# Two lots of the down projection as seven block products, with the sums on GpSimd

## The chip, the cores and the metric

The kernel runs on one core of one Trainium2 chip. The metric is the device time of one execution, in microseconds (us). Before the change the median of three runs is 1117.38 us (1116.92 to 1117.68). The engines are called as in the profile: PE (TensorE, matmuls), PEld (its weight loads), DVE (VectorE), ACT (ScalarE), POOL (GpSimd) and SP (SyncE, which issues the transfers).

## The reference

Two layers of a bidirectional encoder on 512 tokens of width 1024. A layer has a mixer (12 token heads and 4 heads over 256 memory rows) and a gated feed-forward part with 2816 hidden columns. The change lies in the second.

```python
for i in range(DEPTH):                      # DEPTH = 2; mixer a, then mixer b
    h = rms_norm(x, g_mix_pre[i])
    ...                                     # attention heads, tok and mo
    o = jnp.concatenate([tok, mo], axis=-1) @ w_o[i]
    x = x + rms_norm(o, g_mix_post[i])
    h = rms_norm(x, g_ffn_pre[i])
    gu = h @ w_gate_up[i]                   # (512, 1024) @ (1024, 5632)
    f = (jax.nn.silu(gu[..., :D_FF]) * gu[..., D_FF:]) @ w_down[i]   # (512, 2816) @ (2816, 1024)
    x = x + rms_norm(f, g_ffn_post[i])
```

## The kernel before

**Numbers in two parts.** Every float32 operand of a matmul is split into a high part (rounded, on ACT) and a low part (the rest, on DVE: source minus high part). A product is three matmuls, high x high, high x low and low x high. `split` is this pair of instructions, lines 283 and 287.

**Hidden tiles.** A tile `f` is 128 of the 2816 hidden columns, for all 512 tokens, so a layer has 22. Tiles 0 and 1 are multiplied plainly. The other 20 are made by `body`, with seven block products instead of eight: gate and up weights are the two columns of a 2x2 block matrix, and the tokens fall into two halves of 256. A product is 12 matmuls of 256 columns (line 1026 to 1028), 84 a tile. The products are called A11, A12, S2, nS1, S3, S4, A22, after the forms of the activations, which `Forms.finish` makes once a layer. The weights' forms are made for each tile: `raw` holds the gate block, `rb` the up block, `ru` sums. Pair `a` is split from the gate block as loaded. `load_b` and `prep_c` make three sums of 128x512 (lines 1004, 1005, 1010) and split pair `c`, `prep_b` splits pair `b`, and `prep_d` makes a fourth sum (line 1017) and splits pair `d`. All four sums are on DVE.

**Order in a body.** PE works through S2 and nS1 (pair c of this tile), A11 of the next tile (pair a), S3 (b), A12 of the next tile, S4 (b), A22 (d). Between them ACT copies intermediate sums out of PSUM (`u2`, `p5`, `p1`), and DVE adds them (`c`, lines 1062 and 1070). At the end come silu, the product `s*c` (line 1076) and its split into the hidden tile `f` (lines 1078, 1079).

**Lots and the way down.** Tiles come in lots of 8, 6 and 8. When a lot's tiles stand in SBUF, `down` multiplies them with their rows of `w_down`: for both column halves of 512, for each unit of two tiles (128x1024, split as loaded), for all four token tiles of 128, six matmuls of 512 columns (`down_prod`). Sums of a lot go from PSUM to `o`, by an ACT copy for the first lot and a DVE sum afterwards. The last body of a lot has no next tile, so the first unit of the way down fills those two places (`first`, `second`). The last lot's way down is in `ffn_out`, with the closing norm and the residual. In layer 1 the last token tile's second half is done in two parts of 256 columns (`ending`).

**Buffers and queues.** Split weights lie in a ring of four pairs (`whl`), loaded ones in three `raw`, two `rb` and two `ru` buffers. The order on PE is that of the code; those of the other engines are set by a scheduler when the program is built, and each engine works strictly in that order. SP issues the loads, each waiting for its buffer. `ahead`, called after each unit of `down`, uses idle time to split a weight of layer 1's mixer and to store the pair, by turns a load and a store: eight pairs are wanted, four of `wq` and four of `wo`, and 14 calls in layer 0 make seven in time.

Of the kernel before, what the change touches and what calls it, by code (L numbers as in the profile page):

```python
# [35 lines left out]
LOTS = ((0, 8), (8, 14), (14, 22))  # L36
# [146 lines left out]
class Trunk:  # L183
# [703 lines left out]
    def ffn_out(self, get, w, fs, o, head, gpost, gpre, resid, dst, rs):  # L887
# [14 lines left out]

        def ending(t):

# [3 lines left out]
            for z in range(2):  # L908
                ps = self.tagged(("acc", "s")[z])[:, :256]
                for u in range(nu):  # L910
                    for k in (2 * u, 2 * u + 1):
                        c = slice((k % 2) * 512 + 256 * z, (k % 2) * 512 + 256 * z + 256)
                        self.mm3(ps, get(0, k, t), get(1, k, t), wu[u][0][:, c], wu[u][1][:, c], k == 0, k == len(fs) - 1)
# [383 lines left out]
```

## Time and profile before

| what | value |
| --- | --- |
| median of three runs | 1117.38 us |
| span of the profiled execution | 1115.4 us |
| PE busy | 1094.4 us, 98% |
| DVE busy | 839.4 us, 75% |
| ACT busy | 661.2 us, 59% |
| POOL busy | 201.4 us, 18% |
| mean granted clock of TensorE | 0.998 |
| transfers | 139.30 MB, mean 125 GB/s |

The page gives the span from first to last instruction and no further time for the profiled execution; the span lies 2.0 us below the runs' median. A row of a timeline has the start and the duration in us, engine, line, operation, output<-inputs and shapes; what stands in brackets is idle time before it and what ended that. A row of a group ends with busy us and mean ns of one, then the idle time before. A busy PE is not PE at its peak, because matmuls overlap in the record.

### The profile page before, as it was taken

The numbers are of one execution on the slowest core, as the hardware profiler recorded it, in microseconds if no ns is written. First come the engines' busy times: TensorE is split into PE (matmuls) and PEld (weight loads), VectorE is DVE, ScalarE is ACT, GpSimd is POOL, SyncE is SP. The second block draws the span as 40 slices with busy tenths as digits, with TensorE's granted clock in tenths as the row PEclk, the third lists the DMA queues.
The fourth block names the chain that finished last, engine by engine and source line by source line (L and its number), as shares of the span: only waits on it lengthen the run. The fifth ranks groups of instructions, "written<-read, shape, count | busy, mean of one in ns | idle before, by whom it ended". The sixth has DMA issues, their size and how long they took to land.

```text
span 1115.4 us, 19564 instructions
## 1 busy us (share of the span) xinstructions
PE 1094.4 (98%) x7487; PEld 1005.2 (90%) x7487; DVE 839.4 (75%) x1401; ACT 661.2 (59%) x1349; POOL 201.4 (18%) x349
## 2 busy tenths in 40 slices
PE   9999999999999999999999999999999999999997
PEld 7889988999889989998898888878999899899986
DVE  5688886899557866885797988758996478669854
ACT  7578984766445534653467888756664356346631
POOL 5693341102000000000343553212000000000001
PEclk9999999999999999999999999999999999999999
DMA  6521025443653382326443221145136123423243
GB/s 239 189 79 51 25 77 189 152 152 115 238 188 112 113 286 76 100 79 210 162 169 114 77 76 39 38 152 188 44 111 225 57 85 114 141 68 101 83 166 114
DMA packets 38686, 139.30 MB, mean 125 GB/s; under 512 B 4416, under 2 KB 4800, under 8 KB 38464
## 3 DMA queue, kind: packets, MB, share of 16 engines
q1 hardware_dynamic: 38448, 137.91, 36.7%
q8 instruction: 59, 0.97, 0.4%
q14 instruction: 35, 0.29, 0.1%
q10 hardware_dynamic: 144, 0.14, 0.0%
HBM read 119.16 MB, written 18.87 MB: 124 GB/s over the span
## 4 chain that ended last, share of the span: by engine, by line
PE 86%; DVE 5%; POOL 3%; ACT 3%; issue 2%; DMA 1%; SPq 0%; DVEq 0%; POOLq 0%; ACTq 0%
PE ps L274 13%; PE ps L275 13%; PE ps L273 13%; PE ps L1028 12%; PE ps L1026 12%; PE ps L1027 12%; PE tp L631 3%; PE o L646 2%; PE o L645 2%; PE s L570 1%; PE s L571 1%; DVE tl L287 1%; DMA raw<-in_wkv_dram 1%; POOL p L621 1%; POOL r L307 1%
## 5 line engine op out<-in xcount | busy, mean ns | idle before, releaser
L283 ACT ACTIVATE whi<-raw 128x1024 fp32r<-128x1024 f32 (+2 forms) x186 | 157.8, 862 | 174.0 <-PE ps L1028 73.7
L287 DVE TENSOR_TENSOR wlo<-raw,whi 128x1024 fp32r<-128x1024 f32 (+2 forms) x178 | 175.3, 996 | 74.5 <-ACT whi L283 70.6
L1027 PE MATMUL ps<-sf,wlo 128*128 128x256 f32 x640 | 179.7, 281 | 0.0
L1026 PE MATMUL ps<-sf,whi 128*128 128x256 f32 x640 | 179.7, 281 | 0.0
L1028 PE MATMUL ps<-sf,whi 128*128 128x256 f32 x640 | 179.7, 281 | 0.0
L273 PE MATMUL ps<-whi,f 128*128 128x512 f32 (+1 forms) x360 | 138.6, 385 | 0.0
L274 PE MATMUL ps<-wlo,f 128*128 128x512 f32 (+1 forms) x360 | 138.5, 385 | 0.0
L275 PE MATMUL ps<-whi,f 128*128 128x512 f32 (+1 forms) x360 | 138.4, 384 | 0.0
L1028 PE MATMUL ps<-a,whi 128*128 128x256 f32 x480 | 134.4, 280 | 0.0
L1026 PE MATMUL ps<-a,whi 128*128 128x256 f32 x480 | 134.3, 280 | 0.0
L1027 PE MATMUL ps<-a,wlo 128*128 128x256 f32 x480 | 133.8, 279 | 0.0
L1027 PEld LDWEIGHTS ps<-sf,wlo 128*128 128x128 f32 x640 | 121.4, 190 | 0.5
L1026 PEld LDWEIGHTS ps<-sf,whi 128*128 128x128 f32 x640 | 121.1, 189 | 0.5
L1028 PEld LDWEIGHTS ps<-sf,whi 128*128 128x128 f32 x640 | 121.4, 190 | 0.0
L316 POOL TENSOR_SCALAR e<-sso 128x1 f32<-128x1 f32 x8 | 3.4, 422 | 563.6 <-ACT junk L311 563.5
L273 PE MATMUL ps<-whi,hT 128*128 128x256 f32 (+1 forms) x320 | 98.7, 309 | 0.4 <-ACT whi L300 0.4
L274 PE MATMUL ps<-wlo,hT 128*128 128x256 f32 (+1 forms) x320 | 93.9, 294 | 2.1 <-DVE wlo L287 1.3
L621 POOL TENSOR_SCALAR p<-p,rd 128x256 f32<-128x256 f32 (+2 forms) x128 | 76.7, 618 | 99.6 <-DVE rd L618 44.8
L275 PE MATMUL ps<-whi,hT 128*128 128x256 f32 (+1 forms) x320 | 93.7, 293 | 0.0
L1027 PEld LDWEIGHTS ps<-a,wlo 128*128 128x128 f32 x480 | 90.5, 188 | 0.2
L1026 PEld LDWEIGHTS ps<-a,whi 128*128 128x128 f32 x480 | 90.5, 188 | 0.2
L1028 PEld LDWEIGHTS ps<-a,whi 128*128 128x128 f32 x480 | 90.1, 188 | 0.0
(205 smaller groups left out, 2738.0 us busy)
## 6 DMA issues: line engine op xcount, KB each, us to landing
raw<-in_wgu_dram SPq DMA_DIRECT2D x48, 512.0 KB, 4.4
raw<-in_wd_dram SPq DMA_DIRECT2D x44, 512.0 KB, 4.4
rb<-in_wgu_dram SPq DMA_DIRECT2D x40, 512.0 KB, 3.6
raw<-in_wo_dram SPq DMA_DIRECT2D x17, 512.0 KB, 3.6
raw<-in_wq_dram SPq DMA_DIRECT2D x16, 512.0 KB, 4.7
xt<-x SPq DMA_DIRECT2D x12, 512.0 KB, 4.4
raw<-in_wm_dram SPq DMA_DIRECT2D x8, 512.0 KB, 3.9
x<-y SPq DMA_DIRECT2D x8, 512.0 KB, 2.9
```

The costliest lines, as they stand in the source:

```text
L273: mm(out, lh, rh, start=first, stop=False)
L274: mm(out, lh, rl, start=False, stop=False)
L275: mm(out, ll, rh, start=False, stop=last)
L283: a = nc.scalar.activation(hi, src, AF.Copy)
L287: b = nc.vector.tensor_sub(lo, src, hi.bitcast(F32))
L621: self.pooled = nc.gpsimd.tensor_scalar(hd["p"][z][:, :n], hd["p"][z][:, :n], rd[:, z:z + 1], 1.0, op0=OP.mult, op1=OP.mult)
L631: nc.tensor.transpose(tp[:, z], hd["p"][i][:, jj * P:(jj + 1) * P], self.ident)
L645: nc.tensor.matmul(o[:, c0:c1], hd["v"](j), th, start=(j == 0), stop=False, skip_group_check=True)
L646: nc.tensor.matmul(o[:, c0:c1], hd["v"](j), tl, start=False, stop=last, skip_group_check=True)
L1026: mm(out, wh[:, s], rh, start=start and k == 0, stop=False, skip_group_check=True)
L1027: mm(out, wl[:, s], rh, start=False, stop=False, skip_group_check=True)
L1028: mm(out, wh[:, s], rl, start=False, stop=k == 3, skip_group_check=True)
```

## The change

Lots have 6, 6 and 10 tiles. For the first two lots the way down is a 2x2 block product of its own: tokens in halves of 256, the lot's tiles in halves of three (`HALF`), the output's columns in halves of 512. Seven products take the place of eight, each of 18 matmuls of 512 columns. In the order of the work they are A11, A12, S2, S1, S3, S4 and A22.

The hidden tiles are needed in more forms. `keep_hidden` stores tiles of a lot's first half as first token half and, negated, a difference (one POOL subtraction of 128x256, line 990). For a tile of the second half POOL makes three sums of 128x256 (lines 997 to 999), which are split as two forms more. The weight blocks are `b11`, `b12`, `b21` and `b22` (128x1536, held as 1024 + 512); `t2` is a fifth buffer for sums. POOL makes the four block sums (`sub`, line 1164). Each product's block is split by `pairs`. `down_begin` stands in the place of `first`, with four of the six steps of A11.

The four sums of gate and up weights for each tile (lines 1048, 1049, 1054, 1061) are issued on POOL instead of DVE. `ahead` is called six times a lot, 12 in all. `ffn_out` now works on ten tiles, and does the first unit of its second half for all token tiles before it loads the last one. The negation of hidden tiles, which body had before, is now in the plain tiles too (`signed`).

```diff
-LOTS = ((0, 8), (8, 14), (14, 22))
+LOTS = ((0, 6), (6, 12), (12, 22))
+HALF = 3
...
-    def down(self, get, w, fs, c, o, head=None):
...
-        wu = [self.unit(w[1, fs[0] // 2 + u]) for u in range(nu)]
+        wu = [self.unit(w[1, u]) for u in range(nu - 1)]
...
+        wu.append(self.unit(w[1, nu - 1]))
...
-        def hidden(i):
+        def slots(i):
             return [f32r(pools["f"], [P, S], f"f{z}{i}") for z in range(2)]
+        def signed(pair, c, src):
+            nc.scalar.activation(pair[0][:, c], src, AF.Copy, scale=-1.0)
+            nc.vector.scalar_tensor_tensor(pair[1][:, c], src, -1.0, pair[0][:, c].bitcast(F32), op0=OP.mult,
+                                           op1=OP.subtract)
+        def keep_hidden(f, s):
+            lot = next(c for c, (f0, f1) in enumerate(LOTS) if f0 <= f < f1)
+            i = f - LOTS[lot][0]
+            p = F[f] = slots(i)
+            a, b = slice(0, 256), slice(256, 512)
+            if lot == len(LOTS) - 1:
+                signed(p, slice(0, 512), s)
+            elif i < HALF:
+                signed(p, a, s[:, a])
+                nc.gpsimd.tensor_tensor(s[:, a], s[:, a], s[:, b], op=OP.subtract)
+                signed(p, b, s[:, a])
+                kept[i] = s
+            else:
+                signed(p, slice(0, 512), s)
+                r = kept.pop(i - HALF)
+                x = temp("q")
+                nc.gpsimd.tensor_tensor(x[:, b], s[:, b], r[:, a], op=OP.subtract)
+                nc.gpsimd.tensor_tensor(x[:, a], s[:, b], r[:, b], op=OP.add)
+                nc.gpsimd.tensor_tensor(r[:, a], s[:, a], x[:, b], op=OP.subtract)
+                F["S12", lot, i - HALF] = v = slots(i + HALF)
+                signed(v, slice(0, 512), x)
+                if (i - HALF) % 2 == 0:
+                    F["S4", lot, (i - HALF) // 2] = slots(3 * HALF + (i - HALF) // 2)
+                q = i - HALF
+                signed(F["S4", lot, q // 2], (a, b)[q % 2], r[:, a])
+        def block(c, name, z, i, t):
+            f0 = LOTS[c][0]
+            key, h = {"A11": (f0 + i, 0), "S3": (f0 + i, 1), "A12": (f0 + HALF + i, 0), "A22": (f0 + HALF + i, 1),
+                      "S1": (("S12", c, i), 0), "S2": (("S12", c, i), 1), "S4": (("S4", c, i // 2), i % 2)}[name]
+            pair = F[key]
+            return pair[z][:, 256 * h + P * t:256 * h + P * t + P]
         def temp(tag, n=512):
-            return tmp.tile([P, n], F32, tag=tag, name=tag, bufs=2 if n == 512 else 1)
+            return tmp.tile([P, n], F32, tag=tag, name=tag, bufs={"c": 2, "s": HALF}.get(tag, 1))
+        def product(f):
+            if f - max(f0 for f0, _ in LOTS if f0 <= f) < 2:
+                return early.tile([P, S], F32, tag="s", name="s", bufs=2)
+            return temp("s")
         def act(f, pg):
-            s = temp("s")
+            s = product(f)
             nc.scalar.activation(s, pg[0], AF.Silu)
-            nc.vector.tensor_mul(s, s, pg[1])
-            F[f] = hidden(f)
-            self.split(F[f][0], F[f][1], s)
+            nc.vector.scalar_tensor_tensor(s, s, -1.0, pg[1], op0=OP.mult, op1=OP.mult)
+            keep_hidden(f, s)
...
-                nc.vector.tensor_add(ru[:, :512], raw[f][:, :512], rb[:, :512])
-                nc.vector.tensor_add(rb[:, :512], rb[:, :512], rb[:, 512:])
+                nc.gpsimd.tensor_tensor(ru[:, :512], raw[f][:, :512], rb[:, :512], op=OP.add)
+                nc.gpsimd.tensor_tensor(rb[:, :512], rb[:, :512], rb[:, 512:], op=OP.add)
-            nc.vector.tensor_add(ru[:, 512:], ru[:, :512], rb[:, 512:])
+            nc.gpsimd.tensor_tensor(ru[:, 512:], ru[:, :512], rb[:, 512:], op=OP.add)
-            nc.vector.tensor_add(raw[f][:, 512:], raw[f][:, 512:], st[f]["ru"][:, 512:])
+            nc.gpsimd.tensor_tensor(raw[f][:, 512:], raw[f][:, 512:], st[f]["ru"][:, 512:], op=OP.add)
...
             nc.scalar.activation(s[:, 256:], x, AF.Silu)
             nc.vector.tensor_mul(s, s, c)
-            F[f] = hidden(pos)
-            nc.scalar.activation(F[f][0], s, AF.Copy, scale=-1.0)
-            nc.vector.scalar_tensor_tensor(F[f][1], s, -1.0, F[f][0].bitcast(F32), op0=OP.mult, op1=OP.subtract)
+            keep_hidden(f, s)
             if nxt is not None:
                 prep_d(nxt)
             st.pop(f)
...
+        tmp = self.pool(temps, f"ft{l}")
+        def raw_block(src, pool, tag, n):
+            t = [pool.tile([P, 1024], F32, tag=tag, name=tag, bufs=n),
+                 tmp.tile([P, 512], F32, tag="rs", name="rs", bufs=5)]
+            if src is not None:
+                nc.sync.dma_start(t[0], src[:, :1024])
+                nc.sync.dma_start(t[1], src[:, 1024:])
+            return t
+        def sub(dst, a, b):
+            for x, y, z in zip(dst, a, b):
+                nc.gpsimd.tensor_tensor(x, y, z, op=OP.subtract)
+        def pairs(t):
+            out = []
+            for x in t:
+                n = x.shape[-1]
+                hi, lo = [self.whl.tile([P, 1024], F32R, tag=z, name=f"w{z}", bufs=4) for z in ("hi", "lo")]
+                self.split(hi[:, :n], lo[:, :n], x)
+                out.append((hi, lo))
+            return out
+        def times(c, ps, name, pr, steps, fresh):
+            mm = nc.tensor.matmul
+            for i, t in steps:
+                lh, ll = block(c, name, 0, i, t), block(c, name, 1, i, t)
+                rh, rl = [pr[i // 2][z][:, i % 2 * 512:i % 2 * 512 + 512] for z in range(2)]
+                mm(ps[t], lh, rh, start=fresh and i == 0, stop=False, skip_group_check=True)
+                mm(ps[t], lh, rl, start=False, stop=False, skip_group_check=True)
+                mm(ps[t], ll, rh, start=False, stop=i == HALF - 1, skip_group_check=True)
+        BY_ROW = [(i, t) for t in range(2) for i in range(HALF)]
+        BY_UNIT = [(0, 0), (1, 0), (0, 1), (1, 1), (2, 0), (2, 1)]
+        def out_of(c, ps, row, col, fresh):
+            for t in range(2):
+                z = o[2 * row + t][:, 512 * col:512 * col + 512]
+                if c == 0 and fresh:
+                    nc.scalar.activation(z, ps[t], AF.Copy)
+                else:
+                    nc.vector.tensor_add(z, z, ps[t])
+        def down_begin(c, h):
+            ws = self.a["ws"][l, c]
+            h["b11"] = raw_block(ws[0, 0], self.wraw, "raw", 3)
+            h["x"] = [self.tagged("acc"), self.tagged("acc")]
+            h["w"] = pairs(h["b11"])
+            h["b21"] = raw_block(ws[1, 0], gu, "rb", 2)
+            h["b12"] = raw_block(ws[0, 1], gu, "ru", 2)
+            h["b22"] = raw_block(ws[1, 1], gu, "rb", 2)
+            times(c, h["x"], "A11", h["w"], BY_UNIT[:4], True)
+        def down(c, h):
+            x, b11, b12, b21, b22 = [h[z] for z in ("x", "b11", "b12", "b21", "b22")]
+            out_of(c, x, 0, 0, True)
+            w = pairs(b21)
+            sub(b11, b12, b11)
+            t2 = raw_block(None, gu, "ru", 2)
+            sub(t2, b22, b11)
+            sub(b12, b22, b12)
+            z = [self.tagged("s"), self.tagged("s")]
+            times(c, z, "A12", w, BY_UNIT, True)
+            out_of(c, z, 0, 0, False)
+            self.ahead()
+            w = pairs(t2)
+            times(c, x, "S2", w, BY_UNIT, False)
+            out_of(c, x, 0, 1, True)
+            sub(t2, b21, t2)
+            self.ahead()
+            w = pairs(b11)
+            y = [self.tagged("pv"), self.tagged("t")]
+            times(c, y, "S1", w, BY_ROW, True)
+            out_of(c, y, 1, 1, True)
+            self.ahead()
+            w = pairs(b12)
+            times(c, x, "S3", w, BY_ROW, False)
+            out_of(c, x, 1, 1, False)
+            self.ahead()
+            w = pairs(b22)
+            times(c, y, "S4", w, BY_ROW, False)
+            out_of(c, y, 0, 1, False)
+            self.ahead()
+            w = pairs(t2)
+            times(c, x, "A22", w, BY_ROW, False)
+            out_of(c, x, 1, 0, True)
+            self.ahead()
         for c, (f0, f1) in enumerate(LOTS):
             fs = list(range(f0, f1))
...
+            last = c == len(LOTS) - 1
             def first():
-                head["w"] = self.unit(self.a["wd"][l][0, f0 // 2])
+                if not last:
+                    down_begin(c, head)
+                    return
+                head["w"] = self.unit(self.a["wd"][l][0, 0])
                 head["ps"] = [self.tagged("acc"), self.tagged("acc")]
                 self.down_prod(head["ps"][0], get, fs, 0, 0, head["w"])
             def second():
+                if not last:
+                    times(c, head["x"], "A11", head["w"], BY_UNIT[4:], True)
+                    return
                 self.down_prod(head["ps"][1], get, fs, 0, 1, head["w"])
                 head["ps"] += [self.tagged("s"), self.tagged("s")]
             for i, f in enumerate(gs):
                 more = gs[i + 1:] + [None, None]
-                body(f, f - f0, more[0], more[1], [first, second])
-            if c < len(LOTS) - 1:
-                self.down(get, self.a["wd"][l], fs, c, o, head)
+                body(f, more[0], more[1], [first, second])
+            if not last:
+                down(c, head)
                 if l == c == 0:
                     self.axial(gu.tile([P, 1024], F32, tag="ru", name="ru", bufs=2))
+        temps.close()
         done()
         return get, fs, o, head
```

What the scheduler made of it is shown at two places. The first is DVE at the end of a layer's first lot. Before, from a split of a down unit to the split of the last hidden tile (`f_4105`; `f_4004` is the one before it, and `c<-ps` are the sums of the bodies):

```order
L287 TENSOR_TENSOR wlo<-raw,whi 128x1024
L1079 SCALAR_TENSOR_TENSOR f_4004<-s,f_4003 128x512
L287 TENSOR_TENSOR wlo<-raw,whi 128x1024
L1062 TENSOR_TENSOR c<-ps,p_4039 128x256
L1070 TENSOR_TENSOR c<-ps,u_4024 128x256
L287 TENSOR_TENSOR wlo<-raw,whi 128x1024 x2
L1076 TENSOR_TENSOR s<-s,c 128x512
L287 TENSOR_TENSOR wlo<-raw,whi 128x1024
L1079 SCALAR_TENSOR_TENSOR f_4105<-s,f_4104 128x512
```

With the change, from the form of the fifth tile (`f_3776<-q`) to the low half of the sixth and last (`f_3901`). Here `raw`, `rb`, `ru` with 1024 columns are b11, b21 and t2, except that the split in row 8 is of the unit loaded by `ahead`; `rs` are the blocks' second parts:

```order
L977 SCALAR_TENSOR_TENSOR f_3776<-q,f_3775 128x512
L977 SCALAR_TENSOR_TENSOR f_3644<-s,f_3643 128x256
L293 TENSOR_TENSOR wlo<-rs,whi 128x512
L293 TENSOR_TENSOR wlo<-rb,whi 128x1024
L1106 TENSOR_TENSOR c<-ps,p_3813 128x256
L293 TENSOR_TENSOR wlo<-rs,whi 128x512
L1114 TENSOR_TENSOR c<-ps,u_3798 128x256
L293 TENSOR_TENSOR wlo<-raw,whi 128x1024
L1120 TENSOR_TENSOR s<-s,c 128x512
L293 TENSOR_TENSOR wlo<-ru,whi 128x1024
L977 SCALAR_TENSOR_TENSOR f_3901<-s,f_3900 128x512
```

Between the two tiles now stand nine instructions where seven stood, and the split of the last tile comes after the first split of t2. On POOL the same stretch had nothing: in a row stood the last norm factor of the mixer's end and the tables of the second mixer.

```order
L321 TENSOR_TENSOR ro<-e,ss_2746 128x1
L322 TENSOR_TENSOR ro<-ro,mhalf 128x1
L316 TENSOR_SCALAR e<-ss 128x1
L321 TENSOR_TENSOR r<-e,ss 128x1
L322 TENSOR_TENSOR r<-r,mhalf 128x1
L663 TENSOR_SCALAR ru<-ru 128x64
L665 TENSOR_TENSOR gt<-ru 128x256 x2
L668 TENSOR_TENSOR gt<-ru 128x4x32 x4
```

Now the forms of the fourth, the fifth and the sixth tile (`q`, `s`) stand there with the block sums between (`ru<-rb,raw` is t2):

```order
L997 TENSOR_TENSOR q<-s 128x256
L998 TENSOR_TENSOR q<-s 128x256
L999 TENSOR_TENSOR s<-s,q 128x256
L997 TENSOR_TENSOR q<-s 128x256
L998 TENSOR_TENSOR q<-s 128x256
L999 TENSOR_TENSOR s<-s,q 128x256
L1164 TENSOR_TENSOR raw<-ru,raw 128x1024
L1164 TENSOR_TENSOR ru<-rb,raw 128x1024
L1164 TENSOR_TENSOR ru<-rb,ru 128x1024
L1164 TENSOR_TENSOR rs<-rs 128x512 x3
L997 TENSOR_TENSOR q<-s 128x256
L998 TENSOR_TENSOR q<-s 128x256
```

The sixth tile's form comes after six block sums. The second place is the start of a layer's lots. On DVE, before, with three sums of tile 2 between the splits of the activations (`a`) and the work of `finish`:

```order
L287 TENSOR_TENSOR wlo<-raw,whi 128x1024
L1004 TENSOR_TENSOR ru<-raw,rb 128x512
L287 TENSOR_TENSOR a_2641<-a_3056,a_2640 128x4x128
L287 TENSOR_TENSOR a_2639<-a_3065,a_2638 128x4x128
L1005 TENSOR_TENSOR rb<-rb 128x512
L1010 TENSOR_TENSOR ru<-ru,rb 128x512
L287 TENSOR_TENSOR a_2641<-a_3112,a_2640 128x4x128
L287 TENSOR_TENSOR a_2639<-a_3121,a_2638 128x4x128
L172 TENSOR_TENSOR s_3218<-a_3065,a_3056 128x512
L174 TENSOR_TENSOR s_3220<-as_2642,a_3056 128x512
L173 SCALAR_TENSOR_TENSOR s_3219<-s_3218,as_2642 128x512
L287 TENSOR_TENSOR sf<-s_3218,sf 128x4x128
```

With the change these three sums stand on POOL, and the three of tile 3 right behind them, which DVE had some 25 to 30 rows later:

```order
L328 TENSOR_TENSOR r<-r,mhalf 128x1
L1048 TENSOR_TENSOR ru<-raw,rb 128x512
L1049 TENSOR_TENSOR rb<-rb 128x512
L1054 TENSOR_TENSOR ru<-ru,rb 128x512
L1048 TENSOR_TENSOR ru<-raw,rb 128x512
L1049 TENSOR_TENSOR rb<-rb 128x512
L1054 TENSOR_TENSOR ru<-ru,rb 128x512
L1061 TENSOR_TENSOR raw<-raw,ru 128x512
L990 TENSOR_TENSOR s<-s 128x256
L1061 TENSOR_TENSOR raw<-raw,ru 128x512
L990 TENSOR_TENSOR s<-s 128x256
```

More of the change, by code (lines that the diff above doesn't have):

```diff
@@ L901, in join, with part @@
             nc.vector.tensor_mul(o[t][:, c], o[t][:, c], g[:, c])
+        def part(z, u):
+            for k in (2 * u, 2 * u + 1):
+                c = slice((k % 2) * 512 + 256 * z, (k % 2) * 512 + 256 * z + 256)
+                self.mm3(tail[z], get(0, k, NT - 1), get(1, k, NT - 1), wu[u][0][:, c], wu[u][1][:, c], k == 0,
+                         k == len(fs) - 1)
         def ending(t):
@@ L908, in ending @@
             for z in range(2):
[L909 to L913, printed above, removed]
+                for u in range(1, nu):
+                    part(z, u)
+                ps = tail[z]
                 c = slice(512 + 256 * z, 768 + 256 * z)
@@ L928, in ffn_out @@
             join(ps[t], t, 0)
-        wu = [self.unit(w[1, fs[0] // 2 + u]) for u in range(nu)]
+        wu = [self.unit(w[1, u]) for u in range(nu - 1)]
+        ps, tail = [], []
+        for t in range(NT):
+            if rs is None and t == NT - 1:
+                for z in range(2):
+                    tail.append(self.tagged(("acc", "s")[z])[:, :256])
+                    part(z, 0)
+            else:
+                ps.append(self.tagged(("s", "pv", "acc", "acc")[t]))
+                self.down_prod(ps[t], get, fs, 0, t, wu[0])
+        wu.append(self.unit(w[1, nu - 1]))
         if rs is not None:
@@ L937, in ffn_out @@
                 break
-            ps = self.tagged(("s", "pv", "acc", "acc")[t])
-            for u in range(nu):
-                self.down_prod(ps, get, fs, u, t, wu[u])
+            for u in range(1, nu):
+                self.down_prod(ps[t], get, fs, u, t, wu[u])
             if rs is not None and t >= 2:
@@ L1041, in p2, with body @@
             seven(f, z, "a", 1, "A12", True)
-            s = st[f]["s"] = temp("s")
+            s = st[f]["s"] = product(f)
             nc.vector.tensor_add(s[:, :256], z, st[f]["p1"])
             nc.scalar.activation(s[:, :256], s[:, :256], AF.Silu)
-        def body(f, pos, nxt, nxt2, fill):
+        def body(f, nxt, nxt2, fill):
             d = st[f]
@@ new lines, in ffn @@
+        BY_ROW = [(i, t) for t in range(2) for i in range(HALF)]
+        BY_TILE = [(i, t) for i in range(HALF) for t in range(2)]
+        BY_UNIT = [(0, 0), (1, 0), (0, 1), (1, 1), (2, 0), (2, 1)]
[4 more added lines that the diff above has]
+                    nc.scalar.activation(z, ps[t], AF.Copy)
+                else:
+                    nc.vector.tensor_add(z, z, ps[t])
```

36 lines of the change are left out of this document (14 added, 22 removed).

## The prediction

> **What bounds the kernel now.** I read the page first, then what TensorE (PE) waits for, then stretches of the feed-forward part, and last single instructions. The page gives busy times, the chain of work that ended last, and mean costs.
>
> ```profile
> PE 1094.4 (98%) x7487; PEld 1005.2 (90%) x7487; DVE 839.4 (75%) x1401; ACT 661.2 (59%) x1349; POOL 201.4 (18%) x349
> PE 86%; DVE 5%; POOL 3%; ACT 3%; issue 2%; DMA 1%; SPq 0%; DVEq 0%; POOLq 0%; ACTq 0%
> ```
>
> PE bounds it, with 86% of the chain. The view of PE's waits names no wait of the feed-forward part longer than a microsecond; its longest rows are in the mixers:
>
> ```profile
> PE tp L631 <- DVE tl L287: 2.6, 7, 0.7
> PE o L645 <- DVE tok L654: 2.4, 5, 0.7
> ...
> PE ps L274 <- DVE wlo L287: 1.3, 2, 0.8
> ```
>
> A matmul's price is its pitch, since matmuls overlap. In the timeline (start, duration) 256 columns take 0.12 us and 512 take 0.23:
>
> ```profile
> 501.00 0.28 PE L1028 MATMUL ps<-sf,whi 128*128 128x256 f32 x1
> 501.12 0.28 PE L1026 MATMUL ps<-sf,whi 128*128 128x256 f32 x1
> ...
> 520.40 0.39 PE L274 MATMUL ps<-wlo,f 128*128 128x512 f32 x1
> 520.63 0.39 PE L275 MATMUL ps<-whi,f 128*128 128x512 f32 x1
> 520.86 0.39 PE L273 MATMUL ps<-whi,f 128*128 128x512 f32 x1
> ```
>
> A hidden tile made by seven products (84 matmuls) is thus 10.1 us of PE. Two stretches, start of layer 0's feed-forward part and its first bodies, show how near VectorE (DVE) is to becoming the bound (columns: length, then PE, PEld, DVE, ACT, POOL busy, clock):
>
> ```profile
> 213.90:233.10 19.20, 19.20 (x168) 19.20 (x167) 19.20 (x31) 14.35 (x23) 0.00 (x0) 1.00 0.26 92
> 228.00:268.00 40.00, 40.00 (x339) 40.00 (x339) 38.93 (x58) 25.32 (x44) 0.00 (x0) 1.00 0.43 148
> 268.00:278.80 10.80, 10.80 (x93) 10.80 (x93) 10.50 (x14) 5.84 (x10) 6.10 (x7) 1.00 0.46 137
> ```
>
> DVE is full for 19.2 us, and 97% busy for 40 us; POOL has nothing to do there. The third stretch is the only one in which POOL works beside a body. Its instructions, POOL's first:
>
> ```profile
> 272.89 0.74 POOL L665 TENSOR_TENSOR gt<-ru 128x256 f32<-128x256 f32 x1
> 273.59 1.72 POOL L665 TENSOR_TENSOR gt<-ru 128x256 f32<-128x256 f32 x1
> 275.27 0.91 POOL L668 TENSOR_TENSOR gt<-ru 128x128 f32<-128x128 f32 x1
> ...
> 271.50 1.23 DVE L287 TENSOR_TENSOR wlo<-raw,whi 128x1024 fp32r<-128x1024 f32 x1 [0.30 <-ACT whi L283]
> 272.64 0.42 DVE L1070 TENSOR_TENSOR c<-ps,u 128x256 f32<-128x256 f32 x1
> 272.98 1.73 DVE L287 TENSOR_TENSOR wlo<-rb,whi 128x1024 fp32r<-128x1024 f32 x1
> 274.63 1.22 DVE L1076 TENSOR_TENSOR s<-s,c 128x512 f32<-128x512 f32 x1
> 275.78 0.94 DVE L287 TENSOR_TENSOR wlo<-raw,whi 128x512 fp32r<-128x512 f32 x1
> ```
>
> The split begun at 272.98 takes 1.73 us instead of 1.23: without the excess it would have begun at 273.48, when POOL's first sum was ending. POOL's second sum takes 1.72 instead of 0.74: it got going at 274.57, when that split was ending. The product at 274.63 lasts until 275.85, which is 0.69 (its price, below) after POOL's second sum ended at 275.31, less 0.15 of overlap. A DVE instruction with two SBUF operands and a POOL sum exclude each other here, and take turns one for one. An instruction that reads one operand from PSUM keeps its price (L1070, 0.42). The starts give pitches too: 1.14 us for a 1024-column split (271.50 to 272.64), 0.34 for a PSUM one of 256.
>
> **The change part by part.** Prices, from the groups:
>
> ```profile
> L287 DVE TENSOR_TENSOR wlo<-raw,whi 128x1024 fp32r<-128x1024 f32 x100 | 121.9, 1223 | 73.5 <-ACT whi L283 69.7 <-DMA pair<-wlo 2.8 <-PE ps L1028 0.8
> L1004 DVE TENSOR_TENSOR ru<-raw,rb 128x512 f32<-128x512 f32 x40 | 27.4, 686 | 20.9 <-DMA raw<-in_wgu_dram 11.5 <-DMA rb<-in_wgu_dram 9.4
> L1076 DVE TENSOR_TENSOR s<-s,c 128x512 f32<-128x512 f32 x40 | 27.9, 698 | 0.1
> L1062 DVE TENSOR_TENSOR c<-ps,p 128x256 f32<-128x256 f32 x40 | 16.8, 419 | 2.4 <-PE ps L1028 2.4
> L1078 ACT ACTIVATE f<-s 128x512 fp32r<-128x512 f32 x40 | 25.1, 627 | 6.7 <-DVE s L1076 6.5
> L273 PE MATMUL ps<-whi,f 128*128 128x512 f32 x344 | 134.1, 390 | 0.0
> 32.39 1.27 POOL L285 TENSOR_TENSOR wlo<-raw,whi 128x512 fp32r<-128x512 f32 x1
> ```
>
> *Matmuls.* Each lot of six takes 126 matmuls instead of 144. With the last lot's ten tiles, matmuls of 512 columns fall from 1032 (344 for each of three lines) to 954, and the 256-column ones of the closing tile rise from 48 to 60: -78 x 0.23 + 12 x 0.12 = **-16.5 us**, all on the bounding engine.
>
> *Sums of gate/up.* Four DVE sums a tile go (0.69 each, 160 in all, 110 us of DVE) and four POOL sums come, of which L285 is the nearest row (same size, alone): 1.27 us, 5.1 a body. POOL's 256-column sum is 0.74 by L665, and a 1024-column one I estimate at 2.5, twice 1.27. In a plain body DVE then has three long splits, three 512-column operations and three PSUM ones: 3.7 + 2.1 + 1.3 = 7.0 us, and 5.1 of POOL takes turns with 5.8 of it. If each POOL sum delays DVE in full, DVE needs 12.1 us of 10.1; if the sums fall in DVE's gaps, 7.0. In the middle of a lot I think the gaps suffice: before, each wait of DVE is for PE or ACT, and weights are split some 2 to 5 us before use. Cost 0, bound 0 to 2 us a body.
>
> *Start of each layer.* Here there are no gaps (19.20 of 19.20). The order puts six POOL sums in a row and then four more, beside `finish`, which is all two-operand work. PE needs tile 2's c pair at 233.06; before, DVE ended it at 232.48:
>
> ```profile
> 230.67 0.68 DVE L287 TENSOR_TENSOR sf<-s,sf 128x512 fp32r<-128x512 f32 x1
> 231.27 1.21 DVE L287 TENSOR_TENSOR wlo<-ru,whi 128x1024 fp32r<-128x1024 f32 x1
> ...
> 233.06 0.28 PE L1026 MATMUL ps<-sf,whi 128*128 128x256 f32 x1
> ```
>
> DVE loses three sums (-1.8 at the pitch of 0.60 from 230.67 to 231.27) and waits for up to seven POOL sums of about 1.2 (+8.4): 6.6 late, less 0.6 slack, 6.0. At least 0, if POOL is done before `finish` begins. I take 5, since turns were one for one in every row: **+10 us** for two layers (0 to 12).
>
> *End of each six-tile lot.* This is the largest term. Let 0 be the start of the lot's last body. PE would end that body at 11.3 (five gate/up products of 1.44 and the 18 matmuls of A11 at 0.23), start A12, and come to its third tile, which needs the low half of this body's hidden tile, at about 14.3 (13 matmuls on). On DVE, in order, stand ahead of that half: splits of b11, b21, the unit loaded ahead and t2 (1024 columns, pitch 1.14), six operations of 512 (0.6), one of 256 and two PSUM ones (0.34): 4.6 + 3.6 + 1.0 = 9.2 us, from the product of the fifth tile at about 1.5 on. On POOL are ready from the same time: three sums of 256, then three of 1024 and three of 512 for the blocks, then one of 256 for the last tile's form: 2.8 + 7.5 + 3.8 = 14.1. Turn by turn, 1.5 + 9.2 + 14.1 = 24.8, less about 2 where a PSUM operation or the last POOL sums run alone: 22.8, so PE waits 8.5 us in three pieces: for b11's second part, for c's first half, and for the third tile. If POOL never delayed DVE, the low half still follows the body's end at 11.3 by silu, product, t2's split, the ACT cast (0.63) and 0.69: 15.0, a wait of 0.7. Then S2's product needs the second part of t2, which stands behind two sums into o, with POOL's last 1024-column sum between: 0 to 2.4, I take 1. Per lot 9.5 (0.7 to 11), the row's one-for-one turns deciding; four lots: **+38 us** (3 to 44). [...] By full blocking without the 2 us of overlap each lot's end would wait 10.5, and the kernel would come out 8 later, at 1160; the rows show the exclusion, but also the overlap of 0.15 a turn, so I keep 8.5. Only layer 0's two lots and layer 1's first have a unit ahead; the difference (1.1) is inside the range.
>
> *Three forms a tile in the second half of a lot.* POOL gets three sums of 256 after the tile's product, DVE 0.69 + 0.42 more, and ACT's copy p5 and the c split queue behind them. PE needs p5 for S4 at 7.2 of the next body; by turns it comes at 6 to 7, and `c` before A22 about 0.5 late. Six bodies: **+3** (0 to 10).
>
> *Down's new work behind it.* Fourteen sums into o instead of eight (0.68 each, PSUM) and 31 split units instead of 22 a layer run beside 28.8 us of PE a lot; DVE has 12 to 17 us there, so their cover is down's own matmuls. `ahead` is called 12 times, not 14, so one pair fewer is stored, and the second mixer splits one more unit (1.2 of DVE, 1.1 of ACT): 0, at most 1.2. SP's stores and loads keep their order, and b22's load, behind one load ahead, is needed some 8 us after its buffer is free: 0. The ten-tile end loads its last unit later, under 4 us of matmuls: 0.
>
> Sum: -16.5 + 10 + 38 + 3 = +34.5 on a span of 1115.4, so 1149.9; the runs' median stood 2.0 above that span, which makes 1151.9, say 1152. The ends: -16.5 + 0 + 3 + 0 = -13.5 and -16.5 + 12 + 44 + 10 = +49.5.
>
> **The rivals.** *Faster: the exclusion costs little.* The third stretch speaks for it: 6.10 us of POOL in one body, DVE at 10.50 of 10.80, and PE lost nothing. If at lot ends POOL's sums ran before DVE's queue fills, 2.5 a lot and 1 a layer start would remain: -16.5 + 10 + 2 = -4.5, 1113; with the low ends, 1104. It decides below 4 us a lot with no late start. Against it: POOL's block sums can't start before b11 is split, which is when DVE's queue fills.
>
> *DVE and POOL together become the bound of every body.* With 0.7 us lost in each of 40 and 2 in the twelve with three forms, +28 - 3 + 24: 1201. Against it: gaps exist once four sums have left.
>
> [...]
>
> **How the numbers follow.** A difference under 0.2% (2.2 us) can't be told from none. Turns at the starts and ends of lots, as summed: 0.62 (1128 to 1168 on its own). Little exclusion: 0.20, of which 0.04 falls within 0.2%. DVE/POOL bound everywhere: 0.09. Lower clock: 0.09. The first keeps 0.01 for a gain and 0.01 for no change. Hence faster 0.16 + 0.01 = 0.17, same 0.04 + 0.01 = 0.05, slower 0.60 + 0.18 = 0.78. The range leaves out the lowest part of the second and most of the third: 1106 to 1176.
>
> **What would show it.** Right: PE's waits name the hidden low half and the split of a block's second part at each lot's end, 2 to 4 us each, four times; block splits on DVE last over 1.5 us where POOL is busy; the start of a layer waits for the c pair. Wrong: DVE's splits keep 1.23 us beside POOL, or POOL's block sums are over before DVE's queue begins; PE's busy time falls by 16 us with no wait in place.

## The result and the profile after

The changed kernel takes 1196.18 us (median of 4 runs, 1195.69 to 1197.23) against 1117.31: a ratio of 1.0705 (95% interval 1.069 to 1.072), 79 us slower. The prediction was slower too, at 1152, and its range ended at 1176. The profiled execution took 1195.69 with a span of 1193.9.

The busy times of the page, then the view of what PE waits for (in all, times, longest):

```profile
PE 1109.7 (93%) x7421; PEld 1007.8 (84%) x7421; DVE 948.5 (79%) x1335; ACT 691.3 (58%) x1419; POOL 612.2 (51%) x589
```

```profile
PE ps L1181 <- DVE wlo L293: 28.9, 11, 5.5
PE ps L1070 <- DVE c L1106: 12.5, 10, 1.9
PE ps L1070 <- ACT p L1076: 5.4, 6, 1.8
PE ps L1182 <- DVE f L977: 5.1, 4, 2.4
PE ps L280 <- DVE a L293: 4.2, 2, 2.1
```

PE has 66 records fewer and is busy 15 us longer: its mean granted clock fell from 0.998 to 0.979. And it now waits for DVE: for a block's split (L1181), for the sums `c` in the bodies (L1106), for the last hidden tile (L977), for the activations (L280). Five stretches of layer 0's feed-forward part show where: bodies of the first lot, its end with the way down, the same for the second lot, and the bodies of the ten-tile lot (length, then PE, PEld, DVE, ACT, POOL busy, clock):

```profile
216.02:276.70 60.68, 52.95 (x423) 51.73 (x422) 52.08 (x63) 33.50 (x58) 30.65 (x21) 0.97 0.31 97
276.70:322.77 46.07, 37.43 (x162) 29.94 (x162) 36.52 (x32) 21.05 (x31) 30.36 (x22) 0.89 0.49 167
322.77:390.88 68.11, 60.35 (x470) 58.83 (x469) 51.78 (x55) 35.87 (x63) 45.69 (x31) 0.95 0.32 102
390.88:437.42 46.54, 37.38 (x162) 29.34 (x162) 42.85 (x39) 19.21 (x27) 33.02 (x20) 0.93 0.43 145
437.42:533.75 96.33, 96.18 (x806) 95.97 (x805) 88.97 (x88) 55.72 (x96) 68.95 (x35) 1.00 0.32 98
```

The last row has the four POOL sums per tile as well, and PE loses nothing there. Taking each stage's length from the first matmul's start to that of the next stage, less its matmuls at the pitch of the kernel before (0.119 for 256 columns, 0.228 for 512), gives this table for every kernel of the study (us, layer 0 / layer 1; the pitch is a little shorter in layer 1, which the row of before shows):

| kernel | bodies, lot 1 | end, lot 1 | bodies, lot 2 | end, lot 2 | bodies, lot 3 |
| --- | --- | --- | --- | --- | --- |
| before | -0.2 / -1.2 | -0.1 / -0.2 | 0.0 / -1.0 | -0.1 / -0.2 | 0.1 / -1.4 |
| the change | 10.7 / 11.2 | 13.3 / 13.0 | 12.3 / 6.1 | 13.7 / 11.4 | 0.6 / -1.1 |
| gu_dve | 3.5 / 4.2 | 18.6 / 13.4 | 0.1 / -0.7 | 13.3 / 12.7 | 0.1 / -1.8 |
| blk_dve | 10.5 / 11.2 | 9.9 / 8.6 | 10.1 / 6.0 | 11.7 / 10.0 | 0.5 / -0.2 |
| forms_dve | 8.8 / 8.4 | 13.3 / 13.5 | 7.5 / 3.6 | 11.3 / 13.0 | 0.5 / -0.4 |
| all_dve | 0.3 / 0.2 | 8.3 / 4.3 | 0.1 / -1.0 | 10.9 / 6.8 | 0.1 / -1.8 |
| old_gu_pool | 6.1 / 5.0 | 0.1 / -0.2 | 0.2 / -0.7 | -0.1 / -0.1 | 0.1 / -0.6 |
| best5 | 0.3 / 0.2 | 0.3 / 0.4 | 2.2 / -1.0 | 3.1 / 3.2 | 0.1 / -1.8 |

Less the row of before, the change loses 43 us in the bodies of its six-tile lots and 52 at their ends: -16.5 + 43 + 52 = 78.5, the whole difference of the spans (1193.9 - 1115.4). (The -16.5 is the count of matmuls at their pitch.)

The end of layer 0's first lot in the timeline (start, duration), DVE first, then POOL:

```profile
276.37 1.23 DVE L977 SCALAR_TENSOR_TENSOR f<-s,f 128x512 fp32r<-128x512 f32 x1
278.88 2.92 DVE L977 SCALAR_TENSOR_TENSOR f<-q,f 128x512 fp32r<-128x512 f32 x1 [1.28 <-ACT f L976]
281.72 2.55 DVE L977 SCALAR_TENSOR_TENSOR f<-s,f 128x256 fp32r<-128x256 f32 x1
284.20 2.82 DVE L293 TENSOR_TENSOR wlo<-rs,whi 128x512 fp32r<-128x512 f32 x1
286.95 1.21 DVE L293 TENSOR_TENSOR wlo<-rb,whi 128x1024 fp32r<-128x1024 f32 x1
...
278.15 0.74 POOL L999 TENSOR_TENSOR s<-s,q 128x256 f32<-128x256 f32 x1
278.85 2.40 POOL L1164 TENSOR_TENSOR raw<-ru,raw 128x1024 f32<-128x1024 f32 x1
281.33 2.67 POOL L1164 TENSOR_TENSOR ru<-rb,raw 128x1024 f32<-128x1024 f32 x1
283.96 2.52 POOL L1164 TENSOR_TENSOR ru<-rb,ru 128x1024 f32<-128x1024 f32 x1
```

Turns, as forecast: three DVE instructions that cost 0.4 to 0.7 alone take 2.9, 2.6 and 2.8 us, each ending just after a block sum of POOL. The third is the split of b11's second part, and PE waits 5.5 us for it.

In a body, a tile's form looks like this (layer 0's second lot; rows of four engines, picked out in order of time):

```profile
357.88 0.41 DVE L977 SCALAR_TENSOR_TENSOR f<-s,f 128x256 fp32r<-128x256 f32 x1
358.36 0.74 POOL L990 TENSOR_TENSOR s<-s 128x256 f32<-128x256 f32 x1 [0.96 <-DVE f L977]
359.14 0.42 ACT L976 ACTIVATE f<-s 128x256 fp32r<-128x256 f32 x1 [2.44 <-POOL s L990]
359.59 1.03 DVE L977 SCALAR_TENSOR_TENSOR f<-s,f 128x256 fp32r<-128x256 f32 x1 [1.30 <-ACT f L976]
360.81 2.05 DVE L293 TENSOR_TENSOR wlo<-ru,whi 128x1024 fp32r<-128x1024 f32 x1 [0.19 <-ACT whi L289]
362.78 0.41 DVE L1106 TENSOR_TENSOR c<-ps,p 128x256 f32<-128x256 f32 x1
363.24 0.39 PE L1070 MATMUL ps<-a,whi 128*128 128x256 f32 x1 [1.67 <-DVE c L1106]
```

DVE stands still for 1.30 us until POOL and then ACT have done their part; the next split takes 2.05 us beside POOL; the sum `c` behind both is late. One loss among the bodies is of another kind, at the start of layer 0's second lot:

```profile
314.83 0.39 POOL L669 TENSOR_SCALAR ru<-ru 128x64 f32<-128x64 f32 x1 [9.40 <-DMA ru<-in_qk_norm_g_dram]
320.81 2.15 POOL L1048 TENSOR_TENSOR ru<-raw,rb 128x512 f32<-128x512 f32 x1
325.58 1.06 ACT L289 ACTIVATE whi<-ru 128x1024 fp32r<-128x1024 f32 x1 [6.01 <-POOL ru L1054]
327.18 0.39 PE L1070 MATMUL ps<-a,whi 128*128 128x256 f32 x1 [2.85 <-ACT o L1192]
```

POOL waits 9.4 us for a load and then makes the second mixer's tables, and the gate and up sums of the next lot's first tile stand behind them. ACT waits 6.0 us for the last of these, and PE 2.85 us for the copy of `o` behind that. With half clock after it (6.83 us from 328.18), the first 108 matmuls of this lot take 6.6 us longer than at their pitch, before a tile of the lot has a form. Layer 1 has no such tables and loses nothing there, nor does gu_dve below, with these sums on DVE.

### The profile page after: what moved, and what is told of

Its sections match the earlier page's. It is cut to its first block, busy times and chain, and to the rows that moved or that the text cites. A ratio compares the mean times of both kernels' runs of the same rounds, so it can differ in the third digit from the quotient of the medians.

```text
span 1193.9 us, 19949 instructions
## 1 busy us (share of the span) xinstructions
PE 1109.7 (93%) x7421; PEld 1007.8 (84%) x7421; DVE 948.5 (79%) x1335; ACT 691.3 (58%) x1419; POOL 612.2 (51%) x589
## 5 line engine op out<-in xcount | busy, mean ns | idle before, releaser
L293 DVE TENSOR_TENSOR wlo<-raw,whi 128x1024 fp32r<-128x1024 f32 (+2 forms) x164 | 185.8, 1142 | 47.3 <-ACT whi L289 46.3
L289 ACT ACTIVATE whi<-raw 128x1024 fp32r<-128x1024 f32 (+2 forms) x172 | 142.3, 841 | 101.2 <-PE ps L1072 42.0
L1070 PE MATMUL ps<-sf,whi 128*128 128x256 f32 x640 | 185.1, 289 | 7.8 <-ACT p L1076 5.4
L1071 PE MATMUL ps<-sf,wlo 128*128 128x256 f32 x640 | 183.8, 287 | 0.0
L1072 PE MATMUL ps<-sf,whi 128*128 128x256 f32 x640 | 183.2, 286 | 0.0
L1070 PE MATMUL ps<-a,whi 128*128 128x256 f32 x480 | 136.3, 284 | 15.6 <-DVE c L1106 12.5
L1070 PEld LDWEIGHTS ps<-sf,whi 128*128 128x128 f32 x640 | 125.4, 196 | 12.0 <-ACT p L1076 7.0
L1071 PEld LDWEIGHTS ps<-sf,wlo 128*128 128x128 f32 x640 | 125.3, 196 | 0.6
L1072 PEld LDWEIGHTS ps<-sf,whi 128*128 128x128 f32 x640 | 125.3, 196 | 0.0
L1070 PEld LDWEIGHTS ps<-a,whi 128*128 128x128 f32 x480 | 90.8, 189 | 18.6 <-DVE c L1106 15.3
L1048 POOL TENSOR_TENSOR ru<-raw,rb 128x512 f32<-128x512 f32 x40 | 62.4, 1560 | 76.8 <-DMA rb<-in_wgu_dram 40.3
L1181 PE MATMUL ps<-wlo,f 128*128 128x512 f32 x168 | 70.2, 418 | 29.0 <-DVE wlo L293 28.9
L293 DVE TENSOR_TENSOR wlo<-ru,whi 128x1024 fp32r<-128x1024 f32 x52 | 80.1, 1540 | 21.1 <-ACT whi L289 19.6
L1061 POOL TENSOR_TENSOR raw<-raw,ru 128x512 f32<-128x512 f32 x40 | 74.3, 1859 | 42.8 <-DVE wlo L293 28.5
L280 PE MATMUL ps<-wlo,hT 128*128 128x256 f32 (+1 forms) x320 | 94.0, 294 | 1.9 <-DVE wlo L293 1.1
```

Of the source, the lines that this page charges most:

```text
L280: mm(out, lh, rl, start=False, stop=False)
L289: a = nc.scalar.activation(hi, src, AF.Copy)
L293: b = nc.vector.tensor_sub(lo, src, hi.bitcast(F32))
L1048: nc.gpsimd.tensor_tensor(ru[:, :512], raw[f][:, :512], rb[:, :512], op=OP.add)
L1061: nc.gpsimd.tensor_tensor(raw[f][:, 512:], raw[f][:, 512:], st[f]["ru"][:, 512:], op=OP.add)
L1070: mm(out, wh[:, s], rh, start=start and k == 0, stop=False, skip_group_check=True)
```

## The experiments

**The disputed cost by itself.** Added behind the last result of the kernel before: sums from constant tiles, of DVE and POOL alone and beside each other, and then PE streams with waits between.

```diff
+dve(6, 1024)           # nc.vector.tensor_tensor(d1, a1, b1, op=OP.add), six times; again() sets b1 between the parts
+again()
+pool(6, 512)           # nc.gpsimd.tensor_tensor(g1, a1, b1, op=OP.add)
+again()
+dve(6, 1024)
+pool(6, 512)
...
+for k in (0, 1, 1, 1, 2, 2, 2, 3, 3, 3, 4, 4, 4):   # k sums of 512 on DVE, then 66 matmuls that wait for them
...
```

> The kernel before with a measuring stretch behind its last result; nothing of it is in the output. In it POOL sums of 512 columns run beside DVE instructions of one kind at a time: sums of two SBUF operands (1024 and 512 columns), sums with one PSUM operand, scalar operations with one SBUF operand, and beside ACT copies. Then PE streams of 14 us with waits for DVE of about 1.8, 2.4, 3.0 and 3.6 us between them. Turns: beside POOL a DVE sum of 1024 columns takes 1.2 + 1.3 = 2.5 us from start to start and a POOL sum the same; a PSUM operand leaves both at 0.7 and 1.3; ACT is not touched; of the one-operand kind no row says anything. Rival, slowed by sharing and not excluded: both are stretched a little, under 1.5 times. Clock: waits that fill more than about half of a window of 3.41 us are followed by half clock for one window, the short ones are not.

Merged rows of its timeline (start, duration of the whole row; x is the count): DVE alone, beside six POOL sums of 512, with a PSUM operand beside six more, with one SBUF operand beside six more, and 512 columns beside four POOL sums of 1024; then POOL in the same order (alone first, the fifth row beside ACT copies).

```profile
1113.20 7.46 DVE L1282 TENSOR_TENSOR bd<-ba,bb 128x1024 f32<-128x1024 f32 x6
1131.11 12.23 DVE L1282 TENSOR_TENSOR bd<-ba,bb 128x1024 f32<-128x1024 f32 x6
1145.69 10.12 DVE L1282 TENSOR_TENSOR bd<-ps,bb 128x512 f32<-128x512 f32 x14
1157.10 14.33 DVE L1302 TENSOR_SCALAR bd<-bb 128x1024 f32<-128x1024 f32 x12
1181.98 16.76 DVE L1282 TENSOR_TENSOR bd<-ba,bb 128x512 f32<-128x512 f32 x12
...
1121.93 7.96 POOL L1286 TENSOR_TENSOR bg<-ba,bb 128x512 f32<-128x512 f32 x6 [11.45 <-DVE bb L1278]
1131.15 13.31 POOL L1286 TENSOR_TENSOR bg<-ba,bb 128x512 f32<-128x512 f32 x6 [1.27 <-DVE bb L1278]
1145.73 7.98 POOL L1286 TENSOR_TENSOR bg<-ba,bb 128x512 f32<-128x512 f32 x6 [1.27 <-DVE bb L1278]
1157.14 10.10 POOL L1286 TENSOR_TENSOR bg<-ba,bb 128x512 f32<-128x512 f32 x6 [3.44 <-DVE bb L1278]
1172.77 7.99 POOL L1286 TENSOR_TENSOR bg<-ba,bb 128x512 f32<-128x512 f32 x6 [5.53 <-DVE bb L1278]
1182.03 11.08 POOL L1286 TENSOR_TENSOR bg<-ba,bb 128x1024 f32<-128x1024 f32 x4 [1.27 <-DVE bb L1278]
```

Two SBUF operands: 12.23 instead of 7.46, POOL 13.31 instead of 7.96. The single rows start every 2.20 us on both engines (alone 1.26 and 1.34; 2.5 was forecast), strictly in turn; the sum of both would be 2.60, so 0.4 of a turn overlaps. A PSUM operand and ACT leave POOL at 7.98 and 7.99. The one-operand kind, for which nothing was forecast, takes turns as well: 0.69 alone, 1.66 from start to start beside POOL. In both kinds it is exclusion, not stretching; why the one-operand kind is excluded too no run here shows.

**Sums back to DVE, one kind at a time.** Each edit replaces the engine of some sums:

```diff
-nc.gpsimd.tensor_tensor(...)
+nc.vector.tensor_tensor(...)   # gu_dve: L1048, 1049, 1054, 1061; blk_dve: L1164; forms_dve: L990, 997-999; all_dve: all
```

> The four sums of gate/up per tile go back to DVE; the block product, its block sums and the hidden forms on POOL stay. Turns (POOL sums and DVE instructions with two SBUF operands exclude each other): the 10 us of waits at the two layer starts and their 3 us of lowered clock go, half of the 20 us in the bodies goes, the lot ends stay at about 50: 1165 to 1175. Rival, DVE simply has too much new work (forms, splits of the blocks), wherever the sums run: DVE gets 2.8 us more per body in twelve full bodies of a lot with forms, 1205 or more.

> Only the four block sums of a lot (1024 + 512 columns each) go from POOL to DVE. Turns: at a lot's end 12 us of POOL give way to about 5.2 us of DVE ahead of the last tile, so the waits there fall from 9 to about 4 us and most of the lowered clock with them: 4 x 7 = 28 less, about 1168. Rival, DVE has too much work: 7 us more of DVE per lot where it is full, 1205 to 1224.

> The change with the sums of the hidden forms (one of 256 columns for a tile of a lot's first half, three for one of the second) on DVE instead of POOL; gate/up and block sums stay on POOL. Turns: a body with three forms has 2.2 us less of POOL and 1.0 more of DVE, so half of the 20 us of waits in the bodies goes, and at a lot's end the block sums start 2.8 us earlier: 1170 to 1180. Rival, DVE has too much work: slower than the change by the 1 us per body, 1200 or more.

> All sums (gate/up, blocks, hidden forms) on DVE; POOL has none in the feed-forward part. Turns: no instruction is lengthened any more, DVE's split of 1024 columns stays at 1.2 us everywhere; DVE needs about 2 us a body too much in the bodies with three forms, and 5 us at a lot's end: 1125 to 1145. Rival, DVE has too much work: slower than the change as it is, over 1196.

Measured: gu_dve 1167.74 (ratio 1.0462, 1.0446 to 1.0477), blk_dve 1183.53 (1.0598, 1.058 to 1.0616), forms_dve 1182.47 (1.0585, 1.0565 to 1.0604), all_dve 1131.77 (1.0134, 1.0119 to 1.0149). Each makes the kernel faster although DVE gets more work, so the rival "too much DVE work" falls as the cause of the 79 us; what all_dve still loses is looked at below. The sizes were right for gu_dve and all_dve and missed for the other two: with POOL still busy beside it, the queue's next split is the late one. In blk_dve PE still waits up to 5.7 us for t2's split, and a lot's end falls from 13 to 10 us, not to 6. The three single steps gain 28, 13 and 14 us, together 55; all at once gain 64.

What DVE was doing in the bodies is told by the groups of the change, and the same of all_dve (busy, mean ns | idle before):

```profile
L1120 DVE TENSOR_TENSOR s<-s,c 128x512 f32<-128x512 f32 x40 | 50.3, 1256 | 0.0
L977 DVE SCALAR_TENSOR_TENSOR f<-s,f 128x256 fp32r<-128x256 f32 x36 | 28.9, 804 | 17.3 <-ACT f L976 17.3
L977 DVE SCALAR_TENSOR_TENSOR f<-q,f 128x512 fp32r<-128x512 f32 x12 | 23.0, 1920 | 14.4 <-ACT f L976 14.2
```

```profile
L1120 DVE TENSOR_TENSOR s<-s,c 128x512 f32<-128x512 f32 x40 | 27.4, 685 | 0.2
L977 DVE SCALAR_TENSOR_TENSOR f<-s,f 128x256 fp32r<-128x256 f32 x36 | 15.0, 417 | 0.0
L977 DVE SCALAR_TENSOR_TENSOR f<-q,f 128x512 fp32r<-128x512 f32 x12 | 8.2, 684 | 0.0
```

Two things stand there. The product costs 1256 ns instead of 685, by turns. And DVE is parked 31.7 us in all, in front of a form's low half: that instruction needs POOL's sum and then ACT's rounding of it, and DVE, which works in order, holds the next tile's splits and the sums `c` behind it. With the sums on DVE both go.

**The kernel before with the gate/up sums on POOL.**

> The kernel before with its old lots and old way down; only the four gate/up sums per tile move from DVE to POOL. Turns: the bodies hold (POOL and DVE just fit, as in the ten-tile lot of the change), the two layer starts lose 10 us of waits and about 3 us of lowered clock, nothing else: 1127 to 1133. Rival, DVE has too much work: DVE is relieved by 110 us and nothing is lost, 1117 or below. Third, that POOL and DVE bound every body: 1145 or more.

1131.44 (1.0131, 1.0116 to 1.0146). Only the first lots' bodies lose (6.3 and 6.2 in the table, less the row of before), most of it at the layer starts. PE waits there for a plain tile's weight split (`wlo`) and then for a split of the activations (`a`):

```profile
PE ps L274 <- DVE a L287: 4.2, 2, 2.1
PE ps L275 <- DVE wlo L287: 2.5, 2, 1.3
```

So POOL and DVE do not bound every body: behind the layer starts, where DVE has no form to make, four sums on POOL cost next to nothing.

**The clock.** Up to the last matmul, half clock stands in the change's trace for 47.8 us (ten stretches, 39.6 us of matmuls in them). In warm22, 22 matmuls without use fill PE's wait of 5.5 us in each of the four lot ends.

```diff
+for _ in range(22): nc.tensor.matmul(idle, block(c, "A11", 0, 0, 0), h["w"][0][0][:, :512], start=True, stop=True)
 times(c, head["x"], "A11", head["w"], BY_UNIT[4:], True)
```

> The change with 22 matmuls whose sum nobody reads (5.0 us at 0.23) ahead of the last two steps of A11, where PE waits 5.5 us in each of the four lot ends; DVE's order changes by one neighbour there, that of POOL, ACT and the loads by nothing. The wait stays but PE is busy in it, so the clock should not fall behind it. After those waits PE works 3.6, 5.5, 2.8 and 4.4 us at half clock in the change. If all that is lost there counts, 8 us less: 1188. If DVE's next late split takes it back, because DVE and POOL set the pace of the lot's end anyway, 0 to 3 less: 1193 to 1196.

Half clock fell to 20.5 us (five stretches), and the time to 1193.34 (1.0688, 1.0674 to 1.0703), an interval that overlaps the change's. Counted without the added matmuls, the four lot ends are 12.9, 13.0, 12.5 and 12.9 us longer than their own matmuls at the pitch, against 13.3, 13.7, 13.0 and 11.4 in the change. So behind a late split there the slow matmuls run in time that DVE and POOL need anyway. What the other half-clock stretches cost wasn't tried.

**Can the block product gain at all?** From all_dve on, only DVE's order at the lot ends was changed, step by step.

```diff
 h["w"] = pairs(h["b11"])   ->   with self.urgent(): ...        # best1: b11's splits ahead of the fifth tile's forms,
-self.ahead()                                                   # the first two units ahead come two products later
 sub(b12, b22, b12)         ->   behind S2 (best1), behind S1 (best2)
 sub(t2, b21, t2)           ->   behind S3 (best2)
 pairs(b12), pairs(t2)      ->   with self.urgent(): ...        # best4; t2's only where a lot adds into o
-self.todo = [("wq", ...) ...]   +self.todo = []                # best5: nothing taken ahead for the second mixer
```

> All sums on DVE as in the run with that name; b11's pairs are split ahead of the fifth tile's forms, b22 - b12 is made behind the product S2, and the first two units taken ahead in a lot's way down come two products later. Turns (what is left are places in DVE's queue at the lot ends, about 21 us of waits and up to 8 of lowered clock): the waits for b11 go (4 x 2.1), half of those for t2's second part and the clock with them: 1108 to 1120. Rival, DVE has too much work in the lot as a whole: the waits move to the next block, 1127 to 1135.

> As the run with all sums on DVE and b11's pairs early, but b22 - b12 is made behind the product S1 and b21 - t2 behind S3, each after the split that PE waits for next. Turns gone, what is left are places in DVE's queue: the wait for b11's difference in S1 (2.3 to 2.8 us in each of four lots) and the half clock behind it go, the wait for t2's split in the lots that add into o stays: 1128 - 4 x 2.5 - 4 = 1114 (1110 to 1121). Rival, DVE's work in the whole lot's end is the bound: the waits move on to S3 and A22 and the time stays at 1125 to 1130.

> As the last run, with two places of DVE's queue changed: both parts of the block for S3 are split ahead of the next block's, and where a lot adds into o, the block for S2 is split ahead of the last tile's forms. Turns: the waits at those places go (1.8 in three of four lots, 2.2 and 2.2 in the lots that add into o, with two or three half-clock windows of 1.7): 1122 - 8 - 4 = 1110 (1107 to 1118), below before. Rival, DVE's work at a lot's end is the bound: the waits only change their place, 1119 to 1124.

> As the run beside it, and nothing is taken ahead for the second mixer: no unit of it is split and stored during the way down of layer 0, the mixer splits them itself. At a lot's end in layer 0 DVE and ACT have 3 splits fewer and the ring of split pairs is left to the blocks. Turns: layer 0 loses the same as layer 1 (4 us less), the second mixer needs up to 6 us more, or none where it has room: 1107 to 1114. Rival: the mixer pays more than the lots gain, slower than the run beside it.

best1 1128.10 (1.0102, 1.0085 to 1.0119): the wait for b11 went, and PE waits for b11's difference instead, as the rival said. best2 1122.20 (1.0038, 1.0024 to 1.0051): just above its forecast (1110 to 1121) and below its rival. best4 1121.40 (1.0038, 1.0025 to 1.0051): again only the place moved, as the rival said. best5 1114.19 (0.9978, 0.9969 to 0.9987; 11 runs): faster than both kernels, than the one before by 0.2%. Its page and PE's longest waits in the feed-forward part:

```profile
PE 1084.0 (97%) x7421; PEld 991.4 (89%) x7421; DVE 919.7 (83%) x1573; ACT 688.7 (62%) x1421; POOL 211.0 (19%) x357
```

```profile
PE ps L1182 <- DVE f L977: 2.4, 2, 1.2
```

No stretch of half clock is left up to its last matmul, and PE is busy 10.4 us less than before the change. Since the last step dropped something the kernel before has too, that was tried alone:

> The kernel before, with nothing taken ahead for the second mixer (its old lots, way down and sums on DVE). It tells whether the gain of the last run comes from the block products or from that alone. If the block products gain: 1117 to 1123, since the second mixer then splits seven pairs more itself. If taking ahead was a loss in any case: below 1116.

1119.37 (1.0023, 1.0013 to 1.0033): the kernel before loses 2.7 us by it. So best5's gain does not come from dropping the units ahead: against its like it is some 5 us (ratios of 0.9978 and 1.0023). Taking units ahead pays beside the plain products and costs 7 us beside the block products; that the ring of four split pairs is the reason (a block takes two places, a unit ahead a third) was argued from the order, not shown. In all, of the 79 us that the change lost, 64 go with the sums back on DVE, 10 with DVE's order at the lot ends, and 7 with the units ahead.

## Why the prediction was wrong

- **Matmuls, -16.5: right.** The table closes with it to the microsecond, and best5 shows PE's busy time 10.4 us lower once most of the waits are gone.
- **Sums of gate/up, 0 in a plain body: right** (0.6 and -1.1 in the ten-tile lot). One ground given for it was misread: "each wait of DVE is for PE or ACT", but the quoted row of L1004 has 20.9 us of waits for loads.
- **Layer starts, +10: nearly right, at another place.** 12.5 in the first lots of old_gu_pool. The waits are not for tile 2's c pair but earlier, 1.3 us for a plain tile's weight split and 2.1 for the activations' split: POOL began while DVE still did the norm (`h`, L786) and these splits.
- **Lot ends, +38: mechanism right, size 52, above the 44 given as its end.** The third tile of A12 came 23.2, 24.5, 23.2 and 25.3 us after the last body's start, where the working said 22.8: 39 us of waits instead of 34, most of each in one piece for b11's second part (5.5). The tail was the smaller: t2's second part and what follows cost 8 us in all instead of 4, and in two of the ends the matmuls behind it ran at half clock (1.7 each).
- **Tiles with forms, +3: the step that failed.** 43 less the starts' 12.5 is 30 us. Of these 6.6 are the start of layer 0's second lot, where the sums stand behind the mixer's tables in POOL's queue; the working had no such term. The other 24 are in the bodies with forms. The working gave a form half a microsecond by turns. It left out that the form's sum on POOL stands in a chain DVE, POOL, ACT, DVE, and that DVE is parked for it (31.7 us in all); and it took "the gaps suffice" for these bodies too, from one without forms, where 5.1 us of POOL and 5.8 of DVE's two-operand work already come to more than PE's 10.1. By the bodies of forms_dve the gate/up sums without the forms cost 18 over before beside the starts (4 of them at that second lot's start). By those of gu_dve the forms without the gate/up sums cost 9.5, all but 0.4 of it in the first lots. So in a lot with forms the gate/up sums do not fit, and the forms alone fit in the second lots. How much of the 24 is the chain and how much the turns was not separated.
- **The rivals.** "Little exclusion" is refuted (a pair every 2.20 us, in turn). "DVE and POOL bound every body" came out near the time, 1201, for a reason that the ten-tile lot refutes. The lower clock, given 0.09, did come (47.8 us of half clock up to the last matmul), but warm22 shows that in the lot ends it hardly set the time. It also stood behind windows that were far from idle (PE busy 1.20 of 3.41 us; the last section).

## What to carry to other kernels

Here DVE's work was a queue of float32 operations from SBUF, and a sum moved to POOL was not free time: it took DVE's turn, 2.2 us for a pair that DVE alone does in 2.0 (1.26 + 0.73 in the measuring stretch), and a chain that goes DVE, POOL, ACT and back parked DVE's whole queue (31.7 us in all). So before sums are moved, time such a pair side by side and follow the chain back. Fewer matmuls count only as far as the splits for them are on time, so first read which split PE reaches next and put it first in DVE's queue. Work that fits in one kind of stage has to be summed again for the stage that has one operation more.

## What was not expected of the hardware

The clock fell after short waits: in the change's trace half clock followed a single wait of 1.8 us (until 238.7; half from 239.44 to 242.85), and did not follow one of 2.4 us (until 1011.5). Windows of the change's first lot end, cut where the trace's clock steps (length, PE busy second, clock after POOL):

```profile
276.99:280.40 3.41, 3.19 (x17) 2.42 (x16) 2.12 (x2) 2.11 (x6) 3.41 (x4) 1.00 0.27 108
280.40:283.81 3.41, 1.20 (x10) 0.88 (x8) 3.41 (x2) 0.96 (x2) 3.33 (x2) 1.00 0.00 0
283.81:287.23 3.42, 0.15 (x1) 0.15 (x1) 3.42 (x3) 0.00 (x0) 2.79 (x3) 0.50 0.00 0
287.23:290.64 3.41, 3.41 (x11) 2.95 (x12) 1.26 (x2) 1.62 (x3) 3.33 (x3) 0.50 0.00 0
290.64:294.05 3.41, 3.41 (x26) 3.18 (x25) 3.29 (x4) 2.23 (x4) 1.27 (x2) 1.00 0.20 77
```

All steps of the clock in this trace lie 3.41 us or a multiple apart. Counted in these windows up to the end of the matmuls, half clock followed each of the ten full-clock windows with PE busy for 0.47 of it or less (here 1.20 of 3.41), and none of those with 0.48 or more. In the measuring stretch it followed a window with 0.40 (1.35 of 3.41, from 1301.00) and not one with 0.46 (1.56 of 3.41, from 1283.93), so no single share divides both traces. Waits of 1.7 us there were never followed by it, of 2.4 us one in three, of 3.2 us three in three, of 3.9 us two in three: the length of a wait alone did not tell.
